# Writing out the first chunks of an mLSTM stage by hand, and loading x first

## The chip, the cores and the metric

One core of a Trainium2 chip runs the whole program. TensorE (PE) multiplies, VectorE (DVE) and ScalarE (ACT) do elementwise work, GpSimd (POOL) masks and copies, and the queue of SyncE (SP) issues every DMA, one after the other in its own order. The metric is the device time of one execution in microseconds: 2707.82 at the median of three runs of the kernel before (2706.67 to 2714.88).

## The reference, cut to what matters

The layer runs two groups of heads on one normalised input and joins them by one output product:

```
h    = rms_norm(x, norm_pre_w)                      # (1, 2048, 1024), float32
proj = h @ w_in                                     # columns split in a GDN and an mLSTM part
g    = gdn_bidir(proj_gdn)   * silu(z)              # 8 heads, gated delta rule, both directions
m    = mlstm_bidir(proj_ml)  * sigmoid(o) * silu(z) # 8 heads, key width 64, value width 128
y    = x + rms_norm(concat[g, m] @ w_out, norm_post_w)
```

One direction of an mLSTM head, chunk by chunk, with decay f and input gate i in stabilised form:

```
num = inter * (q @ C) + W @ v,   W = exp(lw - m) * (q k^T)   # lw masked to the past
den = inter * (q @ n) + sum(W)
h   = num / max(|den|, exp(-m))
C   = dec * C + (weighted k)^T v                              # state for the next chunk
```

## The kernel before, in words

Sequence positions are 16 chunks of 128, in 4 blocks of 4. The program first loads x, normalises and transposes it, and splits it in a high and a low part (hh, hl), so that each float32 product becomes three matmuls. The projections, the triangular inverses and the GDN scan follow up to about 2076 us. Then comes the stage that the change is about, the mLSTM heads (`core`, L1334 on), woven with the first half of the output product (`ahead`, L1171 on).

For each of 8 heads, `states(h)` forms 16 states for both directions (pc on PE, L1257; the update C on DVE, L1263 and L1265). It needs keys (wt, loaded at L1218, spread into zero-padded wk by POOL, L1224) and values (v, L1229). `load_block` (L1271 on) loads for four chunks the queries and keys kq and two broadcast rows of decays, rb and qe; `mask_block` masks rb and multiplies qe by the queries on POOL (L1303, L1311). `weights` makes W of a chunk: pq on PE (L1319), two exponentials E on ACT (L1322), one product on DVE (L1327). A chunk then takes four matmuls pn (L1365 and L1369), a small chain dn on DVE, an output o begun on ACT (L1378) and finished on DVE (L1380), and a square junk on ACT (L1385). One state step of the next head goes with each half of a chunk.

`ahead` is the fill: 14 of the 16 chunks' rows times the first half of w_out, 24 matmuls po (L1168) for each of two column halves. `load_wo` brings each of the 16 pieces of w_out (256 KB, L1143) through three raw buffers wr; ACT casts it to woh (L1144) and POOL or DVE, in turn, subtract for the low part wol (L1145). `load_cat` does the same for a chunk of the GDN output: raw ct (512 KB, L1155, one raw buffer), ch on ACT (L1156), cl on DVE (L1157).

`weave` gives out the fills evenly over the steps of `core`. What sets the order: `manual_schedule` at L1394 names PE and POOL, and these keep the order in which the code is written. SP, DVE and ACT are ordered by a planner that works with modelled times. Before the weave, 20 steps run alone (16 plus DLY, which is 4): the states of head 0 and two chunks.

Of the kernel before, what the change touches and what calls it, by code (L numbers as in the profile page):

```python
# [8 lines left out]
F32 = mybir.dt.float32  # L9
# [6 lines left out]
P = 128  # L16
# [4 lines left out]
DLY = 4  # L21
# [5 lines left out]
def kernel(  # L27
# [55 lines left out]
    nc.sync.dma_start(out=npre, in_=norm_pre_w[0].rearrange("(k p) -> p k", p=P))  # L83
    gnw = const.tile([P, 1], F32, name="gnw")
    nc.sync.dma_start(out=gnw, in_=gdn_norm_w[0].rearrange("(k p) -> p k", p=P))
    nc.vector.tensor_scalar(out=gnw, in0=gnw, scalar1=-1.0, scalar2=None, op0=ALU.mult)
    mnw = const.tile([P, H], F32, name="mnw")
    nc.sync.dma_start(out=mnw, in_=mlstm_norm_w[0].rearrange("(k p) -> p k", p=P))

    def cvec(name, src, n):  # L90
        t = const.tile([P, n], F32, name=name)
        nc.sync.dma_start(out=t, in_=src.partition_broadcast(P))
        return t

    alog = cvec("alog", gdn_a_log[0].rearrange("a h -> (a h)"), U)
    dtb = cvec("dtb", gdn_dt_bias[0].rearrange("a h -> (a h)"), U)
    mgb = cvec("mgb", mlstm_gate_bias[0].rearrange("a h -> (a h)"), 2 * U)

# [77 lines left out]
    with ExitStack() as p1:  # L176
# [326 lines left out]
        with ExitStack() as st_:  # L503
# [5 lines left out]
            with ExitStack() as xs_:  # L509
                xp = xs_.enter_context(tc.tile_pool(name="xp", bufs=2, reuse_waits="tile"))  # L510
                ps_x = xs_.enter_context(tc.tile_pool(name="ps_x", bufs=3, space=PSUM, reuse_waits="tile"))
                for src, n, dst in ((gdn_conv_w, n_gct, gcw), (mlstm_conv_w, n_mct, mcw)):
                    raw = xp.tile([5 * n, P], F32, tag="cwr", name="cwr")
                    nc.sync.dma_start(out=raw, in_=src[0].rearrange("k (t p) -> (k t) p", p=P))
                    pt = ps_t.tile([P, TB], F32, tag="tr", name="pt")
                    nc.tensor.transpose(pt[:, : 5 * n], raw, ident[: 5 * n, : 5 * n])
                    nc.vector.tensor_copy(out=dst, in_=pt[:, : 5 * n])
                for b in range(NB):
                    xs = []
                    for i in range(CB):  # L520
                        r0 = (b * CB + i) * P
                        xt = xp.tile([P, D], F32, tag="xt", name="xt", bufs=2 * CB)
                        nc.sync.dma_start(out=xt, in_=x2[r0 : r0 + P, :])
                        sq = hl[b].rearrange("p k t -> p (k t)")[:, :D]
                        ss = xp.tile([P, 1], F32, tag=f"ss{i}", name="ss")
                        nc.scalar.activation(out=sq, in_=xt, func=AF.Square, accum_out=ss)
                        nc.vector.tensor_scalar(
                            out=ss, in0=ss, scalar1=1.0 / D, scalar2=EPS, op0=ALU.mult, op1=ALU.add
                        )
# [5 lines left out]
                        xs.append(xt)  # L535
# [25 lines left out]
                    nc.scalar.copy(out=grow[:, b * TB : (b + 1) * TB], in_=ps[: 2 * NG, :])  # L561
                    for _ in range(3 * KC + (b == NB - 1)):
                        next(fill, None)
# [564 lines left out]
    with ExitStack() as p2:  # L1128
# [44 lines left out]

        def ahead(ps):

            for e in range(H):
                load_wo(wo, e, (nc.gpsimd, nc.vector))
            parts = load_cat(cp, 0, 0)
            for c in range(NA):
                nxt = load_cat(cp, c + 1, 0) if c + 1 < NA else None  # L1180
                for n in range(ND):
                    po = ps.tile([P, DW], F32, tag="po", name="po")
                    yield from product(po, parts, n, 0, True, True)
                    a = cp.tile([P, DW], F32, tag="acc", name="acc")
                    nc.scalar.copy(out=a, in_=po)
                    nc.sync.dma_start(out=acc_d[:, c, n * DW : (n + 1) * DW], in_=a)
                parts = nxt

        with ExitStack() as st_:
# [40 lines left out]

            def states(h):

                C = Cs[h % 2]
                outer, inner = (0, 3), (1, 2)
                if h == 0:
                    for bs in (outer, inner):
                        load_keys(0, bs)
                        load_values(0, bs)
                        spread_keys(0, bs)
                for t in range(NC):  # L1240
# [3 lines left out]
                    if h + 1 < H and t == NC // 2:  # L1244
                        load_keys(h + 1, outer)
                        load_values(h + 1, outer)
                    if h + 1 < H and t == NC - CB:
# [85 lines left out]
            def core():  # L1333

                items = [(h, NC - 1 - i) for h in range(H) for i in range(NC)]
                ready = []
                load_block(0)
                for i, _ in enumerate(states(0)):
                    if i % 2:
                        yield  # L1340
                mask_block(0)
                load_block(1)
                nxt = weights(*items[0])
                for k, (h, c) in enumerate(items):
# [9 lines left out]
                    next(following, None)  # L1354
# [24 lines left out]
                    next(following, None)  # L1379
# [115 lines left out]
```

## Time and profile before

| | |
|---|---|
| median of three runs | 2707.82 us (2706.67 to 2714.88) |
| profiled execution | 2702.94 us |
| its span, first to last instruction | 2701.1 us |
| PE, DVE, ACT, POOL busy | 95%, 61%, 45%, 37% |
| granted PE clock, mean | 0.984 |
| DMA | 468.16 MB, 173 GB/s over the span |

The busy shares say which engine is short over the whole, and the slices of the page where it is not: PE's row of 40 slices has a 7 first, an 8 and then a 5 about slices 31 and 32 (2025 to 2160 us), and 9 nearly everywhere else. A timeline lists an engine's instructions in order of time, with the idle time before each and what released it. A window gives for a stretch the busy time of each engine, the granted clock, the busy share of the DMA engines and the rate.

### The profile page before, as it was taken

The numbers are of one execution on the slowest core, as the hardware profiler recorded it, in microseconds if no ns is written. First come the engines' busy times: TensorE is split into PE (matmuls) and PEld (weight loads), VectorE is DVE, ScalarE is ACT, GpSimd is POOL, SyncE is SP. The second block draws the span as 40 slices with busy tenths as digits, with TensorE's granted clock in tenths as the row PEclk, the third lists the DMA queues.
The fourth block names the chain that finished last, engine by engine and source line by source line (L and its number), as shares of the span: only waits on it lengthen the run. The fifth ranks groups of instructions, "written<-read, shape, count | busy, mean of one in ns | idle before, by whom it ended". The sixth has DMA issues, their size and how long they took to land.

```text
span 2701.1 us, 49253 instructions
## 1 busy us (share of the span) xinstructions
PE 2572.4 (95%) x16974; PEld 2165.6 (80%) x16974; DVE 1646.5 (61%) x4062; ACT 1215.4 (45%) x3280; POOL 1008.8 (37%) x1497
## 2 busy tenths in 40 slices
PE   7999999999999988999999999999998599999998
PEld 6788878778887877778788888888887599998887
DVE  5547766777767888788525555555554466665333
ACT  6446666666662333334433333333332355555221
POOL 2136656676653233333211111211112455554133
PEclk9999999999999999999999999999999799999999
DMA  4135546565654344444446666666665888875564
GB/s 154 57 94 167 176 152 178 159 184 173 178 157 152 123 142 152 129 153 127 156 134 190 203 204 206 203 201 189 217 200 168 234 241 237 237 215 149 193 193 155
DMA packets 418338, 468.16 MB, mean 173 GB/s; under 512 B 32777, under 2 KB 271273, under 8 KB 418089
## 3 DMA queue, kind: packets, MB, share of 16 engines
q1 hardware_dynamic: 418089, 465.02, 56.7%
q8 instruction: 135, 2.21, 0.3%
q14 instruction: 114, 0.93, 0.1%
HBM read 301.92 MB, written 162.99 MB: 172 GB/s over the span
## 4 chain that ended last, share of the span: by engine, by line
PE 60%; DVE 11%; DMA 10%; issue 10%; POOL 6%; ACT 3%; SPq 1%; POOLq 0%; DVEq 0%; ACTq 0%
PE acc L273 32%; PE po L1168 5%; DVE cacc L584 3%; DMA E<-grow_d 2%; PE ps L1002 2%; PE pn L1369 2%; DMA kv<-kv_d 2%; PE pn L1365 2%; DVE dm L829 2%; DVE tmp L825 2%; PE ps L993 2%; PE ps L1025 2%; PE po L1039 2%; PE po L1038 2%; PE pc L1257 2%
## 5 line engine op out<-in xcount | busy, mean ns | idle before, releaser
L273 PE MATMUL acc<-hh,wh 128*128 128x512 f32 x2048 | 832.9, 407 | 0.0
L273 PE MATMUL acc<-hl,wh 128*128 128x512 f32 x2048 | 826.0, 403 | 0.0
L273 PE MATMUL acc<-hh,wl 128*128 128x512 f32 x2048 | 821.2, 401 | 0.0
L273 PEld LDWEIGHTS acc<-hh,wl 128*128 128x128 f32 x2048 | 387.7, 189 | 72.6 <-issue 1.0
L273 PEld LDWEIGHTS acc<-hh,wh 128*128 128x128 f32 x2048 | 388.3, 190 | 69.7 <-issue 1.2
L273 PEld LDWEIGHTS acc<-hl,wh 128*128 128x128 f32 x2048 | 388.4, 190 | 68.9 <-issue 1.0
L231 POOL TENSOR_TENSOR wl<-wr,wh 128x256 fp32r<-128x256 f32 x256 | 206.5, 820 | 613.2 <-ACT wh L230 486.2
L584 DVE SCALAR_TENSOR_TENSOR cacc<-raw,gcw,cacc 128x512 f32<-128x512 f32 x256 | 212.4, 858 | 78.0 <-ACT cacc L580 37.8
L1168 PE MATMUL po<-woh,ch 128*128 128x512 f32 x512 | 210.3, 411 | 14.3 <-ACT woh L1144 13.5
L1168 PE MATMUL po<-wol,ch 128*128 128x512 f32 x512 | 206.8, 405 | 2.1 <-POOL wol L1145 2.1
L1168 PE MATMUL po<-woh,cl 128*128 128x512 f32 x512 | 206.2, 404 | 0.0
L151 POOL TENSOR_TENSOR rs<-rs,mhalf 128x4 f32<-128x4 f32 x64 | 64.7, 1015 | 375.7 <-DVE rs L148 231.3
L230 ACT CAST wh<-wr 128x256 fp32r<-128x256 f32 (+1 forms) x260 | 97.8, 403 | 221.9 <-DMA wr<-in_w_in_dram 137.9
L715 POOL COPY dg<-T 32x128 f32<-32x128 f32 x256 | 152.3, 595 | 16.4 <-DVE T L705 6.4
L705 DVE SCALAR_TENSOR_TENSOR T<-pk,sc,E 128x256 f32<-128x256 f32 x256 | 109.7, 474 | 47.5 <-PE pk L702 40.9
L875 POOL COPY Z<-ZD 32x256 f32<-32x256 f32 x128 | 91.4, 714 | 115.6 <-DMA Z<-uq_d 72.9
L584 DVE SCALAR_TENSOR_TENSOR cacc<-raw,mcw,cacc 128x512 f32<-128x512 f32 x128 | 99.9, 799 | 41.1 <-ACT cacc L580 21.7
L584 DVE SCALAR_TENSOR_TENSOR kq<-raw,gcw,kq 128x512 f32<-128x512 f32 x128 | 104.1, 818 | 32.5 <-ACT kq L580 23.5
L1168 PEld LDWEIGHTS po<-woh,ch 128*128 128x128 f32 x512 | 97.3, 190 | 28.5 <-ACT woh L1144 14.2
L1030 DVE SCALAR_TENSOR_TENSOR sn<-sn,eGL,ps 128x128 f32<-128x128 f32 x224 | 68.0, 344 | 70.3 <-PE ps L1025 70.3
L1168 PEld LDWEIGHTS po<-wol,ch 128*128 128x128 f32 x512 | 97.2, 190 | 16.3 <-POOL wol L1145 3.4
L1369 PE MATMUL pn<-v,W 128*128 128x129 f32 x512 | 101.2, 280 | 8.1 <-DVE W L1327 8.0
(604 smaller groups left out, 4944.0 us busy)
## 6 DMA issues: line engine op xcount, KB each, us to landing
kv<-kv_d SPq DMA_DIRECT2D x256, 256.0 KB, 3.0
wr<-in_w_in_dram SPq DMA_DIRECT2D x256, 128.0 KB, 2.7
uq_d<-T SPq DMA_DIRECT2D x64, 512.0 KB, 4.0
uq<-uq_d SPq DMA_DIRECT2D x128, 256.0 KB, 4.5
zg_d<-zt SPq DMA_DIRECT2D x64, 256.0 KB, 2.8
E<-grow_d SPq DMA_DIRECT2D x64, 256.0 KB, 5.9
kv_d<-tk SPq DMA_DIRECT2D x64, 256.0 KB, 2.5
Z<-uq_d SPq DMA_DIRECT2D x32, 512.0 KB, 4.5
```

The costliest lines, as they stand in the source:

```text
L151: nc.gpsimd.tensor_tensor(out=rs, in0=rs, in1=mhalf[:, :CB], op=ALU.pow)
L230: nc.scalar.copy(out=hi, in_=raw[:, :, :n])
L231: nc.gpsimd.tensor_tensor(out=lo, in0=raw[:, :, :n], in1=hi.bitcast(F32), op=ALU.subtract)
L273: nc.tensor.matmul(ps, l[:, k % KH, :], r[b][:, k, :], start=(k == 0 and i == 0), stop=(k == KC - 1 and i == 2),)
L584: nc.vector.scalar_tensor_tensor(out=acc, in0=raw[:, t : t + TB], scalar=cw[:, t * n_ct + ct : t * n_ct + ct + 1], in1=acc, op0=ALU.mult, ...
L705: nc.vector.scalar_tensor_tensor(out=T2[d][:, :, i], in0=pk, scalar=sc[:, u, c : c + 1], in1=E[d][:, i].unsqueeze(1).broadcast_to([P, 2, P ...
L715: nc.gpsimd.tensor_copy(out=dg[qs, :, at : at + CB], in_=T2[d][qs, 1, :, qs].rearrange("p c i -> p i c"),)
L825: nc.vector.tensor_tensor(out=tv, in0=L[:, j, j + 1 : 32].unsqueeze(2).broadcast_to([P, n, m_]), in1=M[:, j : j + 1, 0:m_].broadcast_to([P ...
L875: nc.gpsimd.tensor_copy(out=self.Z[bs, :, :, bs], in_=ZD[bs].rearrange("p x (d c) -> p d c x", d=2)[:, :, self.qs],)
L1030: nc.vector.scalar_tensor_tensor(out=sn[d], in0=st[d], scalar=eGL[:, u, c : c + 1], in1=ps[d][:, 2], op0=ALU.mult, op1=ALU.add,)
L1168: nc.tensor.matmul(po, l[:, i, :], r[:, ns], start=(first and i == 0 and j == 0), stop=(last and i == H - 1 and j == 2),)
L1369: nc.tensor.matmul(pn[:, d], W[:, d], v, start=False, stop=True)
```

## The change

It has two parts.

**The mLSTM entry.** DLY is 16 instead of 4, so 32 steps run before the weave: 16 state steps of head 0 and eight chunks. These run in a `manual_schedule` that names all five engines, so SP, DVE and ACT too keep the order of the code there; the weave behind it names PE and POOL, as before. No fill runs in them. Instead a generator `weights_out` goes beside them: each half chunk casts and subtracts one piece of w_out and issues the load three pieces on; at piece 12 of 16 the first `load_cat` follows (load, ch, cl), which `ahead` then takes over. Keys and values of head 0 and the blocks 0 and 1 are all issued at the beginning, keys and values ahead of the blocks. Loads of head 1's keys move to chunks 0 and 5, and its state steps begin only behind chunk 5, more of them per chunk.

**The start.** The loads of x of the first block stand ahead of the six small vectors, and the two conv weights are loaded and transposed behind the first block's gate product.

```diff
-DLY = 4
+DLY = 16
...
+        def weights_out():
...
+            for i in range(3):
+                load(i)
+            yield
+            for i, (e, n) in enumerate(pieces):
...
+                nc.scalar.copy(out=a[:, ns], in_=raws[i])
+                (nc.gpsimd, nc.vector)[n % 2].tensor_tensor(
+                    out=b_[:, ns], in0=raws[i], in1=a[:, ns].bitcast(F32), op=ALU.subtract
+                )
+                if i + 3 < len(pieces):
+                    load(i + 3)
+                if i == len(pieces) - 4:
+                    first.append(load_cat(cp, 0, 0))
+                yield
...
-            for e in range(H):
-                load_wo(wo, e, (nc.gpsimd, nc.vector))
-            parts = load_cat(cp, 0, 0)
+            parts = first.pop()
...
+                for bs in (outer, inner):
+                    load_keys(0, bs)
+                    load_values(0, bs)
                 load_block(0)
+                load_block(1)
+                spread_keys(0, outer)
+                yield
+                spread_keys(0, inner)
+                mask_block(0)
                 for i, _ in enumerate(states(0)):
                     if i % 2:
                         yield
-                mask_block(0)
-                load_block(1)
...
-                    next(following, None)
+                    if k == 0:
+                        load_keys(1, outer)
+                        load_values(1, outer)
+                    if k == 5:
+                        spread_keys(1, outer)
+                        load_keys(1, inner)
+                    if k > 5:
+                        next(following, None)
+                    if 5 < k < NC:
+                        next(following, None)
+                        next(following, None)
...
-            with tc.manual_schedule(engines={mybir.EngineType.PE, mybir.EngineType.Pool}):
-                steps = core()
-                for _ in range(NC + DLY):
+            steps, side = core(), weights_out()
+            ET = mybir.EngineType
+            with tc.manual_schedule(engines={ET.PE, ET.Pool, ET.SP, ET.DVE, ET.Activation}):
+                next(steps)
+                next(side)
+                for i in range(NC + DLY):
                     next(steps)
+                    if i >= NC:
+                        next(side, None)
+                run(side)
+            with tc.manual_schedule(engines={ET.PE, ET.Pool}):
                 weave(steps, fill, 2 * NC * H - DLY, (NA * ND - 1) * H * 3)
...
+                        xs.append(xt)
+                    if b == 0:
+                        load_vectors()
+                    for i, xt in enumerate(xs):
```

Where instructions move, in the order of each engine's program (x3 means three of the same in a row; the line numbers of the kernel after are its own). SP's queue at the entry of the stage, before; zg_d and cat_d are stores of the GDN side:

```order
L804 DMA zg_d_102<-zt 128x512 x3
L1279 DMA kq_22518<-mkq_d_105 64x1024
L1280 DMA kq_22518<-mkq_d_105 64x4x128
L168 DMA cat_d<-zt 128x4x128
L1284 DMA rb<-rv_d 128x512
L804 DMA zg_d_102<-zt 128x512
L168 DMA cat_d<-zt 128x4x128
L1284 DMA rb<-rv_d 128x512
L1291 DMA qe_22524<-in_d 64x512 x2
L1218 DMA wt<-mwk_d_109 128x512 x2
L1229 DMA v<-mv_d_117 128x516 x2
```

and after:

```order
L1254 DMA wt<-mwk_d_109 128x512 x2
L1265 DMA v<-mv_d_117 128x516
L167 DMA cat_d<-zt 128x4x128
L1265 DMA v<-mv_d_117 128x516
L807 DMA zg_d_102<-zt 128x512
L167 DMA cat_d<-zt 128x4x128
L1254 DMA wt<-mwk_d_109 128x512 x2
L1265 DMA v<-mv_d_117 128x516 x2
L1311 DMA kq_22518<-mkq_d_105 64x1024
L1312 DMA kq_22518<-mkq_d_105 64x4x128
L1316 DMA rb<-rv_d 128x512 x2
L1323 DMA qe_22524<-in_d 64x512 x2
```

Keys and values (wt, v) now stand ahead of block 0 (kq, rb, qe) instead of behind it.

SP's queue around the first loads of ct, before:

```order
L1229 DMA v<-mv_d_118 128x516
L1218 DMA wt<-mwk_d_110 128x512
L1229 DMA v<-mv_d_118 128x516
L1143 DMA wr<-in_w_out_dram 128x512 x3
L1155 DMA ct<-cat_d 128x1024
L1279 DMA kq_22520<-mkq_d_105 64x1024
L1280 DMA kq_22520<-mkq_d_105 64x4x128
L1284 DMA rb<-rv_d 128x512 x2
L1291 DMA qe_22526<-in_d 64x512 x2
```

and after:

```order
L1265 DMA v<-mv_d_118 128x516 x2
L1265 DMA v<-mv_d_119 128x516
L1254 DMA wt<-mwk_d_111 128x512 x2
L1188 DMA wr<-in_w_out_dram 128x512
L1158 DMA ct<-cat_d 128x1024
L1311 DMA kq_22518<-mkq_d_105 64x1024
L1312 DMA kq_22518<-mkq_d_105 64x4x128
L1316 DMA rb<-rv_d 128x512 x2
L1323 DMA qe_22524<-in_d 64x512 x2
L1316 DMA rb<-rv_d 128x512 x2
L1158 DMA ct<-cat_d 128x1024
```

The first ct stood behind three pieces wr of w_out and now stands behind all sixteen, of which the last is the one just above it; the second ct stands behind the six loads of block 3 and two of block 4.

ACT's program from the first casts of w_out on, before:

```order
L1144 CAST woh_22742<-wr 128x512
L1322 ACT_TABLE_LOAD
L1322 ACTIVATE E<-rb,cb 128x128 x2
L1144 CAST woh_22742<-wr 128x512
L1322 ACTIVATE E<-rb,cb 128x128 x2
L1144 CAST woh_22752<-wr 128x512
L1322 ACTIVATE E<-rb,cb 128x128 x2
L1156 CAST ch<-ct 128x1024
L1322 ACTIVATE E<-rb,cb 128x128 x2
L1378 ACTIVATE o<-pn,dn 128x128
L1322 ACTIVATE E<-rb,cb 128x128 x2
```

and around the same cast of ct after:

```order
L1202 CAST woh_22908<-wr 128x512
L1159 CAST ch<-ct 128x1024
L1426 ACTIVATE o<-pn,dn 128x128
L1434 ACTIVATE junk,so<-o 128x128
L1202 CAST woh_22908<-wr 128x512
L1354 ACTIVATE E<-rb,cb 128x128 x2
L1202 CAST woh_22958<-wr 128x512
L1354 ACTIVATE E<-rb,cb 128x128 x4
L1159 CAST ch<-ct 128x1024
L1354 ACTIVATE E<-rb,cb 128x128 x2
L1426 ACTIVATE o<-pn,dn 128x128
L1434 ACTIVATE junk,so<-o 128x128
```

The cast ch stood behind three pairs of exponentials and three pieces of w_out, ahead of the first output o; it now stands ahead of the output o of chunk 6, and the second one ahead of that of chunk 7. DVE's program has the two subtracts cl in the same places, each ahead of the chain dn of the same chunk. In PE's program the first po stands behind the pn of all eight chunks and behind six state steps of head 1.

At the start SP's queue had eight small loads, four of x, four weight pieces and four of x; it now has four of x, six small ones, four weight pieces, two small ones and then x of the second block.

## Rows read from the trace of the kernel before

**Rows 1.** Windows: us, busy PE PEld DVE ACT POOL, PEclk, DMA share, GB/s
```profile
2080.00:2120.00 40.00, 18.50 (x111) 17.55 (x112) 11.63 (x32) 8.92 (x23) 15.12 (x18) 0.66 1.04 274
2120.00:2130.00 10.00, 0.84 (x7) 0.53 (x5) 3.15 (x8) 2.62 (x7) 0.00 (x0) 0.72 0.97 222
2160.00:2200.00 40.00, 40.00 (x283) 36.75 (x282) 24.88 (x92) 22.68 (x78) 23.78 (x27) 1.00 0.83 228
```

**Rows 2.** Timeline of PE: start, us, line, op, [idle before, releaser]
```profile
2089.78 8.95 PE L1257 MATMUL pc<-v,wk 128*128 128x129 f32 x60 [13.36 <-POOL wk L1224]
2112.10 0.80 PE L1369 MATMUL pn<-v,W 128*128 128x129 f32 x2 [8.04 <-DVE W L1327]
2130.87 0.79 PE L1168 MATMUL po<-woh,ch 128*128 128x512 f32 x1 [10.03 <-ACT woh L1144]
```

**Rows 3.** Timeline of ACT, same columns
```profile
2106.76 0.62 ACT L1144 CAST woh<-wr 128x512 fp32r<-128x512 f32 x1 [30.58 <-DMA wr<-in_w_out_dram]
2126.81 1.04 ACT L1156 CAST ch<-ct 128x1024 fp32r<-128x1024 f32 x1 [5.98 <-DMA ct<-cat_d]
```

**Rows 4.** Windows of L1365, L1168, L1257 alone: PE, PEld, clock, DMA
```profile
2060.00:2160.00 100.00, 9.56 (x40) 8.35 (x40) 0.78 0.78 211
2060.00:2160.00 100.00, 15.96 (x39) 7.28 (x40) 0.78 0.78 211
2060.00:2160.00 100.00, 16.08 (x100) 14.90 (x100) 0.78 0.78 211
```

**Rows 5.** Timeline of PE, one period of the steady weave
```profile
2160.67 0.38 PE L1319 MATMUL pq<-kq 128*128 128x128 f32 x2
2160.89 0.61 PE L1257 MATMUL pc<-v,wk 128*128 128x129 f32 x4
2161.26 0.48 PE L1168 MATMUL po<-woh,cl 128*128 128x512 f32 x1
2161.81 0.38 PE L1365 MATMUL pn<-C,qe 128*128 128x129 f32 x2
2162.62 0.48 PE L1168 MATMUL po<-wol,ch 128*128 128x512 f32 x1
2163.40 0.38 PE L1319 MATMUL pq<-kq 128*128 128x128 f32 x2
```

**Rows 6.** Lines, 2100 to 2160: operation xcount | busy us, mean ns | idle
```profile
L1144 ACT CAST woh<-wr 128x512 fp32r<-128x512 f32 x16 | 9.6, 613 | 38.9 <-DMA wr<-in_w_out_dram 38.6
L1145 POOL TENSOR_TENSOR wol<-wr,woh 128x512 fp32r<-128x512 f32 x8 | 11.3, 1415 | 29.0 <-ACT woh L1144 28.8
L1156 ACT CAST ch<-ct 128x1024 fp32r<-128x1024 f32 x2 | 2.1, 1036 | 6.0 <-DMA ct<-cat_d 6.0
L1157 DVE TENSOR_TENSOR cl<-ct,ch 128x1024 fp32r<-128x1024 f32 x2 | 2.5, 1226 | 6.9 <-ACT ch L1156 6.9
```

**Rows 7.** DMA, 2060 to 2160: slices; issues, KB each, median us to landing
```profile
GB/s 70 0 88 24 18 206 38 200 272 136 260 376 383 242 180 275 256 336 367 198 242 252 356 261 215 263 229 180 254 158 275 284 305 28 234 93 247 216 162 272
wr<-in_w_out_dram SPq DMA_DIRECT2D x19, 256.0 KB, 4.5
wt<-mwk_d SPq DMA_DIRECT2D x12, 256.0 KB, 7.5
ct<-cat_d SPq DMA_DIRECT2D x3, 512.0 KB, 7.7
```

**Rows 8.** Windows, columns as in rows 1
```profile
2143.00:2148.00 5.00, 4.43 (x14) 3.54 (x15) 1.18 (x1) 1.80 (x3) 2.90 (x2) 0.50 0.43 143
```

**Rows 9.** Timelines of SP's queue and of ACT at the start
```profile
0.81 0.46 SPq L83 DMA_DIRECT2D npre<-in_norm_pre_w_dram  x1
4.84 1.87 SPq L523 DMA_DIRECT2D xt<-in_x_dram  x4
8.91 1.06 ACT L526 ACTIVATE hl<-xt 128x1024 fp32r<-128x1024 f32 x1 [6.83 <-DMA xt<-in_x_dram]
15.13 1.06 ACT L526 ACTIVATE hl<-xt 128x1024 fp32r<-128x1024 f32 x1 [0.43 <-DMA xt<-in_x_dram]
```

More of the change, by code (lines that the diff above doesn't have):

```diff
@@ L82, with load_vectors @@
     npre = const.tile([P, KC], F32, name="npre")
-    nc.sync.dma_start(out=npre, in_=norm_pre_w[0].rearrange("(k p) -> p k", p=P))
     gnw = const.tile([P, 1], F32, name="gnw")
-    nc.sync.dma_start(out=gnw, in_=gdn_norm_w[0].rearrange("(k p) -> p k", p=P))
-    nc.vector.tensor_scalar(out=gnw, in0=gnw, scalar1=-1.0, scalar2=None, op0=ALU.mult)
     mnw = const.tile([P, H], F32, name="mnw")
[L88 to L97, printed above, removed]
+    alog = const.tile([P, U], F32, name="alog")
+    dtb = const.tile([P, U], F32, name="dtb")
+    mgb = const.tile([P, 2 * U], F32, name="mgb")
+    def load_vectors():
+        nc.sync.dma_start(out=npre, in_=norm_pre_w[0].rearrange("(k p) -> p k", p=P))
+        nc.sync.dma_start(out=gnw, in_=gdn_norm_w[0].rearrange("(k p) -> p k", p=P))
+        nc.vector.tensor_scalar(out=gnw, in0=gnw, scalar1=-1.0, scalar2=None, op0=ALU.mult)
+        nc.sync.dma_start(out=mnw, in_=mlstm_norm_w[0].rearrange("(k p) -> p k", p=P))
+        for t, src in ((alog, gdn_a_log), (dtb, gdn_dt_bias), (mgb, mlstm_gate_bias)):
+            nc.sync.dma_start(out=t, in_=src[0].rearrange("a h -> (a h)").partition_broadcast(P))
     n_gct, n_mct = 3 * H, H
@@ L511 @@
                 ps_x = xs_.enter_context(tc.tile_pool(name="ps_x", bufs=3, space=PSUM, reuse_waits="tile"))
[L512 to L517, printed above, removed]
                 for b in range(NB):
@@ L561 @@
                     nc.scalar.copy(out=grow[:, b * TB : (b + 1) * TB], in_=ps[: 2 * NG, :])
+                    if b == 0:
+                        for src, n, dst in ((gdn_conv_w, n_gct, gcw), (mlstm_conv_w, n_mct, mcw)):
+                            raw = xp.tile([5 * n, P], F32, tag="cwr", name="cwr")
+                            nc.sync.dma_start(out=raw, in_=src[0].rearrange("k (t p) -> (k t) p", p=P))
+                            pt = ps_t.tile([P, TB], F32, tag="tr", name="pt")
+                            nc.tensor.transpose(pt[:, : 5 * n], raw, ident[: 5 * n, : 5 * n])
+                            nc.vector.tensor_copy(out=dst, in_=pt[:, : 5 * n])
                     for _ in range(3 * KC + (b == NB - 1)):
@@ L1172, in product, with load @@
                     yield
+        first = []
+        def weights_out():
+            raws = []
+            pieces = [(e, n) for e in range(H) for n in range(ND)]
+            def load(i):
+                e, n = pieces[i]
+                raws.append(cp.tile([P, DW], F32, tag="wr", name="wr", bufs=3))
+                nc.sync.dma_start(
+                    out=raws[i], in_=wout[e * P : (e + 1) * P, n * DW : (n + 1) * DW]
+                )
[3 more added lines that the diff above has]
+            for i, (e, n) in enumerate(pieces):
+                ns = slice(n * DW, (n + 1) * DW)
+                if n == 0:
+                    wos[e] = (
+                        wo.tile([P, D], F32R, name=f"woh{e}"), wo.tile([P, D], F32R, name=f"wol{e}")
+                    )
+                a, b_ = wos[e]
+                nc.scalar.copy(out=a[:, ns], in_=raws[i])
+                (nc.gpsimd, nc.vector)[n % 2].tensor_tensor(
+                    out=b_[:, ns], in0=raws[i], in1=a[:, ns].bitcast(F32), op=ALU.subtract
+                )
+                if i + 3 < len(pieces):
[3 more added lines that the diff above has]
+                yield
         def ahead(ps):
-            for e in range(H):
-                load_wo(wo, e, (nc.gpsimd, nc.vector))
-            parts = load_cat(cp, 0, 0)
+            parts = first.pop()
             for c in range(NA):
@@ L1229, in load_values @@
                     nc.sync.dma_start(out=vs[h, b], in_=mv_d[h][:, b * CB : (b + 1) * CB])
+            outer, inner = (0, 3), (1, 2)
             def states(h):
                 C = Cs[h % 2]
[L1234 to L1239, printed above, removed]
                 for t in range(NC):
```

8 lines of the change are left out of this document (4 added, 4 removed).

## The prediction

> **What bounds the kernel now.** I read the page's shares and slices first, then the stretches by windows, then PE's and ScalarE's (ACT's) timelines in the one stretch that the change rewrites, then the DMA view there, and last the start. PE is busy for 95% of the span (the table), so whatever takes no idle time from PE is worth nothing. The slices show two places where PE is not full: the first slice and the one around 2100 us. The second is the entry of the mLSTM stage. Up to 2076.4 (2089.78 less the wait) PE is busy with the scan's products; then it waits 13.36 us for POOL's key copies, 8.04 us for VectorE's (DVE's) first weights W, and 10.03 us for ACT's cast of a w_out piece [rows 1, 2]. ACT itself waited 30.58 us for the first w_out piece to land and later 5.98 us for a tile ct [rows 3]. In that stretch the DMA engines are saturated: busy share 1.04 at 274 GB/s from 2080 to 2120, still 0.97 up to 2130 [rows 1]. So the stalls carry the names of engines, but behind them stands the amount to be loaded before the steady weave of chunks and w_out products can run; the reader should see that the order of engines can shift PE's idle time about, while only fewer or earlier bytes shorten it.
>
> The times below are worked out against the profiled execution, 2702.94 us with a span of 2701.1; it lies 4.88 us under the median 2707.82, which I add back at the end.
>
> **The yardstick in the old trace.** In the new order PE reaches its first w_out product with eight chunks of head 0 done, six state steps of head 1 and no fill. I look up when the old kernel had done work worth the same. By 2160 it had done 10 chunks (40 matmuls of the line at 4 each), 39 fills and (100 - 60)/4 = 10 state steps of head 1 [rows 4], and from 2160 on PE is full, 40.00 of 40 us [rows 1]. What that is ahead by, at full clock: one chunk period is 2.73 us (2160.67 to 2163.40); it holds pn 0.81 (2161.81 to 2162.62), pq 0.22, pc 0.37 and five fills, which leaves 1.33 / 5 = 0.266 per fill [rows 5]. 39 x 0.266 + 2 x 0.81 + 0.22 + 4 x 0.37 = 13.7 us. The old kernel's equal point is therefore 2160 - 13.7 = 2146.3. Call T the time of the first w_out product in the new kernel; the middle of the change is worth T - 2146.3 plus what PE loses at a low clock after T.
>
> **The middle, part by part.** Removed: the wait of 13.36 us for the keys, mostly. The old SP queue issues rb, kq and qe of block 0 ahead of wt and v; the new one issues wt and v first. I put the first state step at 2081 to 2082. Its products, 60 matmuls, took 8.95 us in one run; with W behind them I put the first weighted product (pn) at 2093 instead of 2112.10 [rows 2].
>
> Added: eight chunks without fill. In the steady weave ACT is busy 22.68 and DVE 24.88 us in 40 us [rows 1], 14.7 periods of 2.73, so 1.55 and 1.70 per chunk. The two casts of a chunk add 2 x 0.61 on ACT [rows 6]: 2.8 us if DVE's part lies beside it, 4.5 if the two are in series, as they partly are (W after the exponentials, the output copy after the reciprocal). I take 3.8 per chunk. PE's own part of it is 0.81 + 0.22, so PE is mostly idle there and the stretch is priced by T alone.
>
> What sets T is the row in ACT's and DVE's written order: the cast of ct (ch) stands in front of chunk 6's output copy, the subtract (cl) in front of its reciprocal chain, and a second ch and cl in front of chunk 7's. PE's first w_out product stands behind all of that. In the old order the first ct was hidden, since it was issued behind only three pieces.
> - Bytes: from 2077 up to and with that ct the new SP queue issues 14,144 KiB (each row's tile in four-byte words, 256 KiB for wt, wr, cat_d and zg_d, 264 for v, 512 for ct, 1152 for a block), 14.48 MB. At 274 GB/s that is 52.9 us, so 2130 if no gap opens [rows 1].
> - Turns of the three raw buffers: a piece needs landing 4.5, cast 0.61, subtract 1.41 on POOL [rows 6, 7]: 6.5 us for three pieces, 2.17 each. Piece 0 stands behind 4.74 MB with its own, 17.3 us, so about 2097 with landing; ct is issued behind the subtract of piece 12, 2097 + 12 x 2.17 + 2 = 2125, and lands in 7.7 [rows 7], 2133. I take 2133.
> - ch 1.04 and cl 1.23 [rows 6]: 2135.3. There is one raw ct buffer, so the second load is issued only now, and SP has six loads of block 3 and two of block 4 to issue ahead of it. Its landing is bounded by 4.5 (the pieces, half its size) and 7.7; I take the middle, 6.2: 2141.5. ch, cl and then chunk 7's W, state update and pc: 2.3 + about 3. T = 2147.
>
> After a starved stretch PE runs at the lower level: 2143 to 2148 shows granted 0.50 with 4.43 us busy [rows 8], after which the rows are at full clock. I charge half of five us, 2.5, at T. The old point 2146.3 has its own such loss inside. Middle: 2147 + 2.5 - 2146.3 = +3.2. Bounds: T from 2138 (4.5 everywhere, no gap) to 2157 (7.7 twice, and 3 us more for SP waiting): -6 to +13.
>
> Hidden at nothing: the loads of head 1's keys (moved to chunks 0 and 5) lie beside a stream that is full anyway and are counted in the bytes; the masks of POOL have eight chunks of slack. The weave is denser by 648/240 against 648/252 fills per step; PE is full there, and nothing changes.
>
> **The start.** The four x loads were issued from 4.84 on behind eight small ones, which begin at 0.81; ACT's first square began at 8.91 after 6.83 of waiting [rows 9]. Now x goes first: 4.0 us earlier. The weight pieces gain only the two conv loads, and x of block 1 still stands behind all that stood ahead of it, four x, eight small ones and four weight pieces, so it gains nothing. ACT has the squares and the scaled copies to do one after the other, so it can use an early start. Bounds 0 and -4.0; block 1's first square already waited 0.43 us for its load [rows 9], so its loads are near the path, and I take -2.5.
>
> Sum: 2702.94 + 3.2 - 2.5 = 2703.6, and at the median 2703.6 + 4.88 = 2708.5, taken as 2708. Own range 2701 to 2716. A measurement of this kernel tells about 0.3%, 8.1 us, from no change, so this is no change.
>
> **Rivals.**
> A, the loads come sooner. For: the DMA view has 2.5 us slices of 376 and 383 GB/s in this stretch [rows 7]. At 380, 14.48 MB takes 38.1 us, 2115; then the engines' 3.8 us decide: chunk 6 at 2097 + 6 x 3.8 = 2120, cl 2122.5, second ct +4.5, T = 2132. Middle 2132 + 2.5 - 2146.3 = -11.8, start -2.5: 2688.6, median 2693.5. Against: the mean over 40 us is 274 with the engines already over 1.0. The Trainium skill's page "DMA: Bandwidth & Descriptors", section "Where 436 GB/s comes from", puts the limit of loads from HBM at about 358 GB/s for a core; by it the bytes would take 40 us. In this trace two single slices pass that limit and the 40 us mean of 274 stays well under it; the sum goes by the mean.
>
> B, SP as the bound, slower. SP issues in written order now, so a load that waits for a buffer holds back all behind it. If a piece needs 7.5 us to land, as the keys' loads wt did [rows 7], the buffers turn in 9.5 us, 3.2 per piece: piece 12 done at 2097 + 38 + 2 = 2137, ct at 2145, cl 2147, second ct 2155, T = 2160. Middle +16.2, start -2.5: 2716.6, median 2721.5. For: ct is issued last of sixteen pieces, while the old order issued it after three. Against: wr's median landing is 4.5 though the queue was full [rows 7]. It decides from T = 2154.4 on, where the sum passes +8.1.
>
> C, only the start gains nothing (ACT is the bound there): 2706.1, median 2711, still no change.
>
> **Chances.** Forecast with C 0.55, A 0.25, B 0.20. Of the forecast's cases a little falls over each edge (T under 2138.2 or over 2154.4), as do cases of A and B short of theirs: faster 0.27, same 0.52, slower 0.21. With A and B at their ends the range is 2692 to 2719.
>
> **What would show it.** Right: the first square near 5 us; first pc near 2082 and first pn near 2093; ACT idle 5 us or more for DMA at ch, twice; DMA share about 1 up to 2130; the first w_out product at 2143 to 2151 and PE full from there, at half clock at first. Wrong: a first w_out product before 2138 (A; ch would not wait), or after 2154 with ACT and POOL waiting for wr piece after piece (B); or PE's start gap unchanged. The scan before 2076 should not move except by the start's shift.

## The result

The changed kernel took 2718.99 us at the median of 12 runs (2715.37 to 2730.27), the kernel before 2704.93 (2699.96 to 2714.88): a ratio of 1.0052, 95% interval [1.0038, 1.0066]. It is slower by about 14 us. The forecast was no change, 2708; the measured time lies outside the forecast's own range (2701 to 2716), at the upper end of the range with the rivals (2719) and close to rival B's 2721.5. Each profiled execution below is compared with the profiled one of before, whose span is 2701.1; that of the changed kernel is 2717.7, 16.6 more.

First the timeline of PE at the scan's end, columns as in [rows 2]; the eight transposes (L161, in the changed kernel L160) are the scan's last work on PE. The kernel before:

```profile
2075.39 1.03 PE L161 MATMUL pt<-ident,ob 128*128 128x128 f32 x8
```

The changed kernel, from there to the first w_out product (L1171) and the first row at full clock behind it:

```profile
2080.15 1.03 PE L160 MATMUL pt<-ident,ob 128*128 128x128 f32 x8
2082.18 0.46 PE L1289 MATMUL pc<-v,wk 128*128 128x129 f32 x2 [1.00 <-POOL wk L1260]
...
2100.08 0.46 PE L1413 MATMUL pn<-C,qe 128*128 128x129 f32 x2
2100.38 0.48 PE L1417 MATMUL pn<-v,W 128*128 128x129 f32 x2
...
2149.28 1.23 PE L1289 MATMUL pc<-v,wk 128*128 128x129 f32 x4 [12.31 <-DVE C L1297]
...
2160.52 0.78 PE L1171 MATMUL po<-woh,ch 128*128 128x512 f32 x1
...
2161.86 0.38 PE L1417 MATMUL pn<-v,W 128*128 128x129 f32 x2
```

The scan ended at 2076.42 before and at 2081.18 after, 4.8 us later in these two executions. The scan's code was not changed, and the kernels below, which have the same code there, ended it from 2076.7 to 2085.0 with the start part and from 2077.9 to 2083.4 without it. I take this as what varies between executions. Counted from the scan's end the first w_out product came after 79.3 us. The forecast had 2147 - 2076.4 = 70.6, rival B 83.6. At 2149.28 the wait behind the first ct ends: PE stood 12.31 us for the state update C, which DVE has behind cl.

The windows of the stage after, columns as in [rows 1]:

```profile
2100.00:2110.00 10.00, 5.65 (x33) 4.97 (x32) 3.83 (x13) 4.58 (x14) 6.12 (x7) 0.86 0.76 244
2110.00:2120.00 10.00, 5.46 (x22) 4.86 (x23) 4.79 (x18) 5.57 (x16) 5.66 (x5) 0.50 0.52 152
2120.00:2130.00 10.00, 2.65 (x12) 2.30 (x11) 1.78 (x6) 2.34 (x7) 6.89 (x8) 0.50 0.86 208
2130.00:2140.00 10.00, 4.17 (x18) 3.58 (x17) 1.58 (x4) 2.65 (x8) 3.69 (x4) 0.50 0.90 262
2140.00:2150.00 10.00, 0.72 (x3) 0.72 (x4) 2.22 (x6) 1.55 (x3) 0.63 (x1) 0.50 1.04 284
2150.00:2160.00 10.00, 5.87 (x24) 5.00 (x23) 5.34 (x14) 5.95 (x17) 4.98 (x5) 0.50 0.60 184
```

Where [rows 1] had a DMA share of 1.04 from 2080 to 2120 and 0.97 up to 2130, the changed kernel has 0.76, 0.52 and 0.86 in the three windows from 2100 to 2130. From 2110 on PE's granted clock is 0.50, with 0.7 to 5.9 us busy of each ten. SP's queue in the same stretch (start, duration of the issues) tells why:

```profile
2105.63 10.61 SPq L1188 DMA_DIRECT2D wr<-in_w_out_dram  x6
2116.29 0.45 SPq L1311 DMA_DIRECT2D kq<-mkq_d  x1
...
2137.34 0.67 SPq L1188 DMA_DIRECT2D wr<-in_w_out_dram  x1
2138.06 0.54 SPq L1158 DMA_DIRECT2D ct<-cat_d  x1
...
2148.54 0.32 SPq L1158 DMA_DIRECT2D ct<-cat_d  x1
```

And ACT's casts of pieces (L1202) and of ct (L1159) there:

```profile
2103.59 0.62 ACT L1202 CAST woh<-wr 128x512 fp32r<-128x512 f32 x1 [4.54 <-DMA wr<-in_w_out_dram]
...
2106.30 0.60 ACT L1202 CAST woh<-wr 128x512 fp32r<-128x512 f32 x1
...
2114.49 0.62 ACT L1202 CAST woh<-wr 128x512 fp32r<-128x512 f32 x1 [2.05 <-DMA wr<-in_w_out_dram]
...
2127.13 0.62 ACT L1202 CAST woh<-wr 128x512 fp32r<-128x512 f32 x1 [5.86 <-DMA wr<-in_w_out_dram]
...
2132.81 0.62 ACT L1202 CAST woh<-wr 128x512 fp32r<-128x512 f32 x1 [0.36 <-DMA wr<-in_w_out_dram]
2146.22 1.04 ACT L1159 CAST ch<-ct 128x1024 fp32r<-128x1024 f32 x1 [12.79 <-DMA ct<-cat_d]
...
2153.72 1.05 ACT L1159 CAST ch<-ct 128x1024 fp32r<-128x1024 f32 x1 [0.67 <-DMA ct<-cat_d]
```

SP needed 10.61 us for six pieces, since each waits for a raw buffer, and nothing behind them could go out: that is the share of 0.52. Then block 2 went out in one lump (from 2116.29), and the next piece landed behind it; ACT waited 5.86 us for it. The first ct was issued at 2138.06, ACT waited 12.79 us for it, and the second, issued 2.3 us after that cast began, was cast at 2153.72. In the kernel before ACT's longest wait for a ct was 5.98 us ([rows 3]).

Some of the waiting for buffers comes from POOL. It keeps the written order, and there the masks of block 1 (rb, qe) stand ahead of the subtract of the piece that ACT cast at 2106.30:

```profile
2105.56 1.67 POOL L1335 TENSOR_SCALAR_AFFINE_SELECT rb<-rb 128x512 f32<-128x512 f32 x2
2107.20 2.61 POOL L1343 TENSOR_TENSOR qe<-qe,kq 64x512 f32<-64x512 f32 x2
2109.89 2.82 POOL L1203 TENSOR_TENSOR wol<-wr,woh 128x512 fp32r<-128x512 f32 x2
```

The piece was cast by 2106.90 and its subtract began 3.0 us later; the next load into the same buffer could go out only behind that, and ACT waited 2.05 us for it, up to 2114.49.

The start, for [rows 9]. One of the small loads on SP's queue in the kernel before:

```profile
2.40 0.58 SPq L92 DMA_DIRECT2D alog<-in_gdn_a_log_dram  x1
```

SP's queue in the changed kernel:

```profile
2.66 0.47 SPq L91 DMA_DIRECT2D npre<-in_norm_pre_w_dram  x1
...
5.38 3.23 SPq L96 DMA_DIRECT2D alog<-in_gdn_a_log_dram  x1
...
9.62 1.97 SPq L211 DMA_DIRECT2D wr<-in_w_in_dram  x4
...
12.52 1.31 SPq L516 DMA_DIRECT2D xt<-in_x_dram  x3
```

ACT's first squares of blocks 0 and 1:

```profile
4.47 1.06 ACT L523 ACTIVATE hl<-xt 128x1024 fp32r<-128x1024 f32 x1 [2.38 <-DMA xt<-in_x_dram]
...
16.23 1.06 ACT L523 ACTIVATE hl<-xt 128x1024 fp32r<-128x1024 f32 x1 [1.38 <-DMA xt<-in_x_dram]
```

And PE's first projection product:

```profile
28.82 0.78 PE L272 MATMUL acc<-hh,wh 128*128 128x512 f32 x1
```

The first square came at 4.47 instead of 8.91. But the six small loads took from 2.66 to 9.57 to issue, with 3.23 us at one of them (0.58 before), behind four loads of x that were still under way; before, the six took 3.1 (0.81 to 3.93). So the weight pieces went out at 9.62 instead of 6.75, and block 1's first square came at 16.23, later than the 15.13 of [rows 9]. Matched product by product, the first projection product (28.82, before 32.96) leads by 4.1 us, and at 70 us the lead is 0.9.

### The profile page after: what moved, and what is told of

Read it like the earlier page. It is cut to its first block, busy times and chain, and to the rows that moved or that the text cites. A ratio compares the mean times of both kernels' runs of the same rounds, so it can differ in the third digit from the quotient of the medians.

```text
span 2717.7 us, 49265 instructions
## 1 busy us (share of the span) xinstructions
PE 2585.0 (95%) x16974; PEld 2175.6 (80%) x16974; DVE 1644.5 (61%) x4062; ACT 1216.3 (45%) x3280; POOL 1012.7 (37%) x1497
## 4 chain that ended last, share of the span: by engine, by line
PE 60%; DMA 11%; DVE 10%; issue 9%; POOL 5%; ACT 3%; SPq 1%; POOLq 0%; DVEq 0%; ACTq 0%
PE acc L272 33%; PE po L1171 5%; DVE cacc L587 3%; DMA E<-grow_d 2%; DMA kv<-kv_d 2%; PE ps L1005 2%; PE pn L1417 2%; PE pn L1413 2%; PE ps L1028 2%; PE ps L996 2%; PE po L1042 2%; PE pc L1289 2%; DVE dm L832 2%; PE po L1041 2%; DVE tmp L828 2%
## 5 line engine op out<-in xcount | busy, mean ns | idle before, releaser
L272 PEld LDWEIGHTS acc<-hh,wh 128*128 128x128 f32 x2048 | 389.1, 190 | 69.9 <-issue 1.2
L1171 PE MATMUL po<-woh,ch 128*128 128x512 f32 x512 | 208.4, 407 | 0.8 <-DVE zt L162 0.8
L1171 PE MATMUL po<-wol,ch 128*128 128x512 f32 x512 | 205.9, 403 | 0.0
L1171 PE MATMUL po<-woh,cl 128*128 128x512 f32 x512 | 205.7, 403 | 0.0
L1289 PE MATMUL pc<-v,wk 128*128 128x129 f32 x480 | 78.8, 294 | 36.7 <-DVE C L1297 16.6
L1171 PEld LDWEIGHTS po<-woh,ch 128*128 128x128 f32 x512 | 96.9, 189 | 14.7 <-DVE zt L162 1.0
```

The source lines that it names most:

```text
L272: nc.tensor.matmul(ps, l[:, k % KH, :], r[b][:, k, :], start=(k == 0 and i == 0), stop=(k == KC - 1 and i == 2),)
L1171: nc.tensor.matmul(po, l[:, i, :], r[:, ns], start=(first and i == 0 and j == 0), stop=(last and i == H - 1 and j == 2),)
L1289: nc.tensor.matmul(pc, wk_of(h, b)[:, i].rearrange("p s k -> p (s k)")[:, d * 64 : d * 64 + P], vs[h, b][:, i, :], start=(d == 0), stop=(d ...
```

## The experiments

The ratio is to the runs of the kernel before on the same chip, with a 95% interval; "first product" is the first w_out product's start, counted from the scan's end in the profiled execution.

| run | ratio | first product |
|---|---|---|
| before | 1 | 41.2 |
| the changed kernel | 1.0052 [1.0038, 1.0066] | 79.3 |
| start alone | 1.0000 [0.9989, 1.0012] | 38.1 |
| entry alone | 1.0054 [1.0039, 1.0068] | 77.8 |
| changed, both ct early | 1.0004 [0.9991, 1.0016] | 67.2 |
| changed, first ct early | 1.0008 [0.9994, 1.0021] | 69.8 |
| changed, SP planned | 1.0052 [1.0033, 1.0071] | 82.2 |
| before with DLY 16 | 1.0024 [1.0011, 1.0037] | 57.7 |
| before, columns first | 0.9999 [0.9989, 1.0009] | 39.6 |
| entry by halves | 1.0024 [1.0012, 1.0036] | 38.8 |
| entry by halves, DVE | 1.0000 [0.9989, 1.0012] | 38.6 |
| columns first, late, DVE | 0.9967 [0.9954, 0.9979] | 40.2 |
| columns first, late, POOL and DVE | 0.9981 [0.9969, 0.9992] | 37.5 |

The part of a profiled execution behind the scan's end (its span less that time) leaves out what the scan varies by: 624.7 us before, 636.5 changed, 625.2 with both ct early, 640.9 with SP planned, 614.1 with columns first, late, on DVE.

**Each part alone.** The start part alone on the kernel before:

> The kernel before with only the loads of x moved ahead of the small vectors (conv weights behind the first gate product). In the trace of the changed kernel the first projection products lead by 4.1 us at 33 us, by 0.9 at 70 us, and trail by 0.7 at 110 us; the end of the scan trails by 4.8. Theory: the lead is given back inside the first 110 us, and the later drift is no work of this part, so this kernel is within 2 us of the kernel before. Rival: the drift of the scan comes from this part, so it is 4 to 5 us slower.

The entry part alone:

> The kernel before with only the mLSTM entry changed (eight chunks in written order, w_out piece by piece beside them). Theory: the whole loss sits here, in the stretch from the scan's end to the first w_out product, so +11 to +14 us against the kernel before, with the first w_out product 78 to 80 us behind the scan's end. Rival (the start or the scan holds a third of it): +7 to +9 us.

Start alone: 2704.76 against 2705.29. The interval, -3.0 to +3.2 us, leaves out the rival's 4 to 5, but it doesn't tell no gain from the 2.5 us of the forecast. Entry alone: 2720.41, so +15.1 (10.6 to 18.4), the whole loss and a little over the 11 to 14 expected. In the entry's trace the first product came at 77.8, where the theory had 78 to 80.

**Both ct early**, on the changed kernel:

```diff
-                if i == len(pieces) - 4:
-                    first.append(load_cat(cp, 0, 0))
+                if i == 0:
+                    got = fetch_cat(0, 0)
+                if i == 5:
+                    first.append(load_cat(cp, 0, 0, got))
+                    got = fetch_cat(1, 0)
+                if i == 11:
+                    first.append(load_cat(cp, 1, 0, got))
```

> The changed kernel, but the first ct is loaded behind piece 3 of w_out and cast with piece 5, the second loaded there and cast with piece 11, instead of behind all sixteen pieces. Theory (ct at the end of SP's written order sets the first w_out product): that product moves from 79 us to about 68 us behind the scan's end, and the kernel is 9 to 12 us faster than the changed one. Rival (the turns of the pieces through three raw buffers, in SP's written order, set it anyway): 72 us or more, and a gain of 0 to 6 us.

2706.71: the loss is gone within the interval (-2.4 to +4.3 us against before), 12 us faster than the changed kernel, with the first product at 67.2. ACT's casts of ct in its trace (the lines of this kernel differ; L1164 is ch, L1176 po):

```profile
2118.10 1.04 ACT L1164 CAST ch<-ct 128x1024 fp32r<-128x1024 f32 x1
...
2135.97 1.04 ACT L1164 CAST ch<-ct 128x1024 fp32r<-128x1024 f32 x1
```

PE's first w_out product in it:

```profile
2150.34 0.49 PE L1176 MATMUL po<-woh,ch 128*128 128x512 f32 x1
```

Neither cast waits any more. The eight chunks are as in the changed kernel, and the pieces are no faster: the casts of pieces 0 and 12 lie at 2106.55 and 2137.52, 2.58 us apiece. So slow turns cost nothing that can be told from noise as long as ct doesn't stand behind them.

**The first ct alone early** (the line with 11 left out, the second ct again in `ahead`):

> The changed kernel with only the first ct loaded behind piece 3 and cast with piece 5; the second stays behind all sixteen pieces. Theory: the loss is the chain first ct, cast, subtract, second ct behind the last piece; without its first half the first w_out product comes 66 to 72 us behind the scan's end, 8 to 12 us faster than the changed kernel. Rival (the second ct at the end, or the last pieces, hold it): 74 us or more, gain under 5 us.

2706.73, 69.8: as good within the intervals. It doesn't isolate the first, though: with the raw buffer free, the planner put the second ct's load and cast ahead of the last pieces by itself (issued at 2127.66, cast at 2136.90, while the casts of pieces ran on to 2154).

**SP planned** (`ET.SP` taken out of the first `manual_schedule`):

> The changed kernel with SP's queue left to the planner in the first eight chunks (PE, POOL, DVE and ACT still in written order). The planner issues the first ct behind seven pieces instead of sixteen and the second block ahead of most pieces. Theory (SP's written order starves the DMA engines, whose busy share was 0.52 from 2110 to 2120, and holds ct back): busy share 0.9 or more over the first 50 us of the stage, and 6 to 12 us faster than the changed kernel. Rival (ACT's and DVE's written order, in which chunk 6 stands behind ct, is what costs): within 3 us of the changed kernel.

2718.44, no gain: the rival held. ACT's casts in its trace:

```profile
2119.79 0.62 ACT L1202 CAST woh<-wr 128x512 fp32r<-128x512 f32 x1 [8.14 <-DMA wr<-in_w_out_dram]
...
2138.42 1.04 ACT L1159 CAST ch<-ct 128x1024 fp32r<-128x1024 f32 x1
...
2147.79 1.04 ACT L1159 CAST ch<-ct 128x1024 fp32r<-128x1024 f32 x1 [2.74 <-DMA ct<-cat_d]
```

The first ct was issued at 2109.91 here, but its cast stands behind piece 12 in ACT's written order and came at 2138.42 without any wait. The planner had issued keys, values and a block of the next heads ahead of the pieces; the share of the DMA engines was 1.07 and 1.06 from 2100 to 2120, and ACT waited 8.14 us for a piece. So leaving SP to the planner is no cure, and here a ct that was loaded early gained nothing, since its cast stayed late. It doesn't clear SP's written order, though: the planner also sent the pieces later. Piece 12 was cast 61.3 us behind the scan's end (2137.91 - 2076.66), in the changed kernel 51.6 (2132.81 - 2081.18). How much of the loss lies in SP's order and how much in that of ACT and DVE is not separated; no run moved ct in one of them alone.

**Eight chunks without fill, planned** (DLY 16 in the kernel before, nothing else):

> The kernel before with DLY alone at 16: eight chunks without fill, but SP, DVE and ACT ordered by the planner and w_out loaded by load_wo as before. Theory (what costs is ct's place in the written order, not the chunks without fill): first w_out product 62 to 68 us behind the scan's end, and the time within 4 us of the kernel before. Rival (eight chunks without fill, most of them at half clock, cost by themselves): 8 us or more slower than before.

2711.16 against 2706.18, +5.0: between the two. With everything left to the planner the chunks without fill cost 5 us; with both ct early the same eight chunks cost nothing that can be told from noise. PE in its trace:

```profile
2135.51 0.48 PE L1168 MATMUL po<-woh,ch 128*128 128x512 f32 x1
2142.75 0.80 PE L1168 MATMUL po<-wol,ch 128*128 128x512 f32 x1 [6.76 <-POOL wol L1145]
```

The first product came earlier than the equal point of before, and then PE waited 6.76 us for a piece.

**Columns first**, on the kernel before (the subtracts of a column go to POOL and DVE in turn):

```diff
-            for e in range(H):
-                load_wo(wo, e, (nc.gpsimd, nc.vector))
+            for n in range(ND):
+                for e in range(H):
+                    load_wo(wo, e, (nc.gpsimd, nc.vector), (n,))
```

> The kernel before, but the sixteen pieces of w_out are loaded by column half (all eight of the first half, then the second), so that the first 24 products need eight pieces and not every second of sixteen. Theory (PE's 13.5 us of waiting for casts of pieces behind 2117 comes from pieces that the first products don't need): 5 to 9 us faster than before. Rival (the entry is bound by all its bytes, whatever their order): 0 to 2 us.

2706.44, no change. But behind the first product the trace showed two waits of PE, 4.60 us for DVE's C and then 12.49, in place of six in the kernel before, the longest 10.03. PE in its trace:

```profile
2138.29 0.40 PE L1170 MATMUL po<-woh,ch 128*128 128x512 f32 x1
2151.17 1.12 PE L161 MATMUL pt<-ident,o 128*128 128x128 f32 x4 [12.49 <-POOL o L154]
```

POOL ahead of that wait's end:

```profile
2147.77 1.26 POOL L1148 TENSOR_TENSOR wol<-wr,woh 128x512 fp32r<-128x512 f32 x1 [1.59 <-ACT woh L1147]
...
2150.08 1.04 POOL L154 TENSOR_TENSOR o<-o,rs 128x512 f32<-128x512 f32 x1
```

POOL keeps the order of the code, and there all its subtracts of w_out stand ahead of the normalising (o, L154) of the first finished block. PE's transposes of o waited for the last piece.

**An entry of my own**, eight pieces of the first half during the states and two chunks, the rest inside the first products; the first ct is loaded behind three pieces and cast with the sixth, and block 1 and the masks of block 0 come later (those edits are not shown):

```diff
+            pieces = [(e, n) for n in range(ND) for e in range(H)]
...
+                    for j, _ in enumerate(product(po, parts, n, 0, True, True)):
+                        if c == 0 and n == 0 and j % 2 == 0:
+                            next(side, None)
...
                 for i in range(NC + DLY):
                     next(steps)
+                    if 4 <= i < NC + DLY and i % 2 == 0:
+                        next(side)
```

> A new entry on the changed kernel: keys and values first, then three pieces, block 0 and ct; the eight pieces of the first column half are cast and subtracted during the state steps and two chunks, in written order; then the weave begins, the second half's pieces inside its first products (DLY 4). Theory (the loads that stand ahead of the first product in SP's order set its time): about 6.6 MB instead of 16.7 stand ahead of it, so it comes 30 to 45 us behind the scan's end, and the kernel is 10 to 25 us faster than before. Rival (what is left is needed soon after, so PE's idle time only moves behind the first product): within 4 us of the kernel before.

The first product came at 38.8, as expected, and the kernel was 7 us slower than before, 2713.31 against 2706.18, more than the rival allowed. PE in its trace:

```profile
2116.95 0.77 PE L1176 MATMUL po<-woh,ch 128*128 128x512 f32 x1
...
2149.02 1.35 PE L1300 MATMUL pc<-v,wk 128*128 128x129 f32 x4 [17.07 <-POOL wk L1271]
```

The idle time had moved behind the first product: 17.07 us for POOL's key copies, which stood behind its subtracts and the masks of a block. With the second half's subtracts on DVE (`nc.vector if i >= H else nc.gpsimd`):

> The entry by halves with the second half's subtracts on DVE instead of in turn on POOL. In its trace the first w_out product came 38.8 us behind the scan's end, but PE waited 17.1 us up to 2149 for POOL's key copies wk, which stood behind subtracts that waited for late pieces. Theory (that wait is the whole loss): 10 to 17 us faster than the entry by halves, so 3 to 10 us faster than the kernel before. Rival (the missing bytes make PE wait for the pieces themselves): a gain of 0 to 5 us over the entry by halves, not faster than before.

2706.58, about 7 us better than the entry by halves: between the two, and not faster than before. Of the 17.07 us, 8.16 stayed, and the wait for block 0's qe early on did too, as PE's timeline shows:

```profile
2112.33 0.80 PE L1427 MATMUL pn<-C,qe 128*128 128x129 f32 x2 [16.03 <-POOL qe L1354]
...
2140.18 0.80 PE L1300 MATMUL pc<-v,wk 128*128 128x129 f32 x2 [8.16 <-POOL wk L1271]
```

**Columns first, the second half late and on DVE**, on the kernel before:

```diff
-                load_wo(wo, e, (nc.gpsimd, nc.vector))
+                load_wo(wo, e, (nc.gpsimd, nc.vector), (0,))
...
-                    yield from product(po, parts, n, 0, True, True)
+                    for j, _ in enumerate(product(po, parts, n, 0, True, True)):
+                        if c + n == 0 and j % 3 == 2:
+                            for m in range(1, ND):
+                                load_wo(wo, j // 3, (nc.vector,), (m,))
+                        yield
```

> The kernel before with the pieces by column half, the second half's pieces emitted inside the first 24 products, and their subtracts on DVE (which the planner orders) instead of in turn on POOL (which keeps written order). In the run with columns first PE ran without a stop of note from 2132 to 2138 and then waited 12.5 us for POOL's o, which stood behind four subtracts that waited for late pieces. Theory (the gain of columns first was lost to that one wait): it goes, and the kernel is 5 to 11 us faster than before. Rival (bytes: PE then waits for woh, W or qe elsewhere): within 2 us of before.

2696.51 against 2705.62, 9 us faster than before: the fastest version here. PE's largest wait behind the first product:

```profile
2131.30 1.23 PE L1263 MATMUL pc<-v,wk 128*128 128x129 f32 x4 [5.45 <-DVE C L1271]
```

The window from 2120 to 2160 of the kernel before, columns as in [rows 1]:

```profile
2120.00:2160.00 40.00, 24.34 (x136) 20.71 (x135) 17.11 (x53) 17.55 (x50) 15.96 (x14) 0.79 0.76 213
```

The same window of this kernel:

```profile
2120.00:2160.00 40.00, 32.46 (x199) 28.99 (x198) 23.47 (x77) 22.45 (x67) 16.15 (x14) 0.91 0.92 254
```

PE is busy 32.46 of these 40 us instead of 24.34, although the scan ended 3.9 us later in this execution, and the 12.49 us of columns first are gone. The bytes to load are the same, but they come sooner: the DMA share is 0.92 at 254 GB/s instead of 0.76 at 213. The same with the subtracts in turn on POOL and DVE:

> The faster kernel (columns first, second half inside the first products), but its subtracts in turn on POOL and DVE again. Theory (POOL's written order, with late pieces ahead of a block's o and masks, is what cost): emitted later, fewer subtracts stand ahead of the first block's o (one instead of four), so part of the gain stays: 2 to 7 us faster than the kernel before, PE waiting 3 to 8 us for POOL's o or qe. Rival (where the pieces are emitted is all that counts, not the engine): as fast as the version on DVE, 9 us faster than before.

2698.48 against 2704.38, 5.9 us faster than before; PE waits 2.00 us for o and 1.93 for qe, as its timeline shows; its longest wait behind the first product is one of 6.93 us for DVE's C.

```profile
2141.14 0.66 PE L161 MATMUL pt<-ident,o 128*128 128x128 f32 x4 [2.00 <-POOL o L154]
...
2147.45 0.49 PE L1371 MATMUL pn<-C,qe 128*128 128x129 f32 x2 [1.30 <-POOL qe L1317]
...
2148.79 0.80 PE L1371 MATMUL pn<-C,qe 128*128 128x129 f32 x2 [0.63 <-POOL qe L1317]
```

It fits the theory, but the two intervals overlap: what POOL still costs here is not separated from nothing. This kernel differs from columns first (0.9999) in the late emission alone, and these two intervals touch as well ([0.9969, 0.9992] and [0.9989, 1.0009]); so the late emission gains something against before, and how the 9 us divide between it and DVE stays open.

## Why the prediction was right or wrong

**No change was forecast, and it was slower.** I gave no change 0.52 and slower 0.21. The 14 us are more than the 8.1 that I called the limit of a measurement, and lie at the price of rival B. That the time falls inside the range is luck twice over. The range reaches 2719 only by the ends of the rivals; the forecast's own, 2701 to 2716, is narrower than the bounds of its terms (-6 to +13 and 0 to -4), which make 2698 to 2721. And the sum started from 2707.82, the median of three runs; from the 2704.93 of twelve the range would have ended at 2716.1.

**The step that failed is T, in the landing of the first ct.** The forecast had turns of "2.17 each", piece 12 done at 2125 and ct landed at 2133. Counted from the scan's end, ct landed 8.4 us later (2146.2 - 4.8 = 2141.4). Piece 0 was 1.8 us later than forecast. The casts of pieces 0 and 12 lie at 2103.59 and 2132.81, 2.43 us apiece, which makes 3.1. Between that cast and the issue of ct at 2138.06 lie 5.25 us instead of 2, since SP had keys, values and two pieces to issue in between: 3.3. The rest of the chain was right: from the first ct's landing to the first product I had 14 us, measured 14.3. T itself, 2155.7 on that count (2160.52 - 4.8) against 2147, lies just inside the bound of 2157 that I had set, so the path was right and its size was not. I had priced the bytes and the turns as two bounds of which the larger counts. In this trace they add in part: while the six pieces waited for buffers the DMA engines were half idle, and the lump behind them then delayed the next pieces. That SP's order alone makes them add isn't shown. POOL's masks, which I had put at nothing, are a part of the turns (3.0 us at one piece); they cost nothing by themselves, since the run with both ct early has them in the same place.

**The steps ahead of T** held roughly: the first state step 1.0 us behind the scan's end (2082.18), sooner than the 4.6 to 5.6 of the forecast, and the first weighted product (pn from v and W) at 2100.38, on that count 2.6 us later than 2093. The DMA share of about 1 up to 2130 did not.

**What the loss is made of.** First product 79.3 us behind the scan's end against 69.9 of the equal point (2146.3 - 2076.4): 9.4. The low clock after T cost under 1 us, not 2.5: the matmul at 2160.52 took 0.78, and by 2161.86 the rows are at full clock. Three waits of about 0.5 us for the state updates follow up to 2173, in which the steps of head 1 stand close. Together that is about 12, and the span's 16.6 less the scan's 4.8 is 11.8, inside the interval of the loss (10.3 to 17.9).

**Rival B** had the time nearly right (T 83.6 against 79.3), and its seed, that a load which waits for a buffer holds back all behind it, is what the share of 0.52 shows. As a cause it falls short: with both ct early the pieces turn no faster, and the loss is gone. What decides is the place of ct, its load, cast and subtract, behind twelve and more pieces in the written order, with one raw buffer for two ct in turn. Which of the queues of SP, ACT and DVE has the larger part in it stays open.

**Rival A** fell: ACT waited 12.79 us at ch, and no ten us of the windows above moved over 284 GB/s, with the share at 1.04. The Trainium skill's page "DMA: Bandwidth & Descriptors", section "Where 436 GB/s comes from", gives about 358 for a core as the limit of loads from HBM; this stage stays under it in windows of ten us, as in the trace of before, where three single slices of [rows 7] lie above it (376, 383 and 367, not two as the forecast says).

**The start**, -2.5 in the sum, is not told from 0 by its run (-0.5, interval -3.0 to +3.2). The trace speaks for less: I had the first square right (4.47 for "near 5"), and said that block 1's x gains nothing; its square comes 1.1 us later, behind small loads that took longer to issue, and of the lead of 4.1 us 0.9 is left at 70 us.

**"the order of engines can shift PE's idle time about, while only fewer or earlier bytes shorten it"** sets two things against each other that go together. Columns first, late, on DVE has the same bytes and gained 9 us by order alone, and with that order the bytes came earlier: 264 GB/s instead of 241 in the 80 us behind the scan's end. The DMA engines were full up to 2130, as the forecast says, but not behind that (a share of 0.76 over 2120 to 2160 in the kernel before). Whether the sooner bytes or the lost wait made the gain is not separated. What was right is that a wait taken away shows up at the next engine, as in columns first and in the entry by halves; the gain came with the order of the pieces and their late place in the code together and, in the fastest version, DVE for the late subtracts.

## What to carry to other kernels

An order written out for every queue makes the last item of any side stream a gate for the main one: before fixing it, ask for each load not only when it can land but also which instruction stands behind its conversion. Price the turns of a small buffer ring together with the bytes that one in-order queue must issue between them, not as two bounds. And look at an engine that keeps written order (POOL here) for work of the main chain that stands behind conversions of late pieces: the first product's time alone said nothing, 38.8 us was slower and 67.2 as fast as 41.2.

## What was not expected of the hardware

Four loads of 512 KB issued first made the small loads behind them slow to issue: one took 3.23 us on SP's queue (3.45 in the run of the start alone), where it had taken 0.58 in the kernel before. What holds it was not tried.

After 50 us at a granted clock of 0.50 (2110 to 2160) PE's rows are at full clock from 2161.86 on; PE had worked from 2158.00 with one stop of 0.44 us. In the kernel before it worked from 2143.01 with one stop of 0.55 us, and all of [rows 8] is at 0.50. What makes the difference was not tried.
